# The first four output blocks of a decoder trunk, row tile by row tile

## The chip, the core and the metric

The kernel runs on one core of a Trainium2 chip. Its engines run beside each other and wait for one another through semaphores: TensorE (PE) multiplies, VectorE (DVE) and ScalarE (ACT) do elementwise work, GpSimd (POOL) some more of it, and SyncE (SP) mostly issues transfers. The metric is the device time of one execution in microseconds (us), the median of several runs. Lower is better.

## What is computed

A small hybrid decoder trunk on 256 tokens of width 2048, batch 1: a recurrent block (RG-LRU), an MLP, an attention block with three dilations, and a second MLP, each behind an RMS norm and with a residual add, and a final norm. Cut to what stands around the change:

```python
def reference(x, mix_norm, mlp_norm, final_norm, mlp_w1, mlp_w2, lru_w_in, ...):
    for i in range(DEPTH):                       # 2
        h = _rmsnorm(x, mix_norm[i])
        if i % N_MIXERS == 0:
            x = x + _rglru_block(h, lru_w_in[j], ...)
        else:
            x = x + _dilated_attention_block(h, ...)
        x = x + _mlp(_rmsnorm(x, mlp_norm[i]), mlp_w1[i], mlp_w2[i])
    return _rmsnorm(x, final_norm)

def _rglru_block(h, w_in, ...):
    xg = jnp.einsum('bsd,de->bse', h, w_in)      # 2048 -> 5120
    xb, gb = xg[..., :D_RNN], xg[..., D_RNN:]
    ...

def _rmsnorm(x, g):
    y = x32 * lax.rsqrt(jnp.mean(x32 * x32, axis=-1, keepdims=True) + EPS)
    return (y * g).astype(x.dtype)
```

The change concerns the first of these products: four blocks of 128 output channels of `w_in` applied to the normed tokens.

## The kernel before

**Three products for one.** Float32 factors are split in two: a high part, rounded for the fast matmul format, and a low part, the rest. A product of a weight block and tokens is hi x hi + hi x lo + lo x hi, three matmuls into the same PSUM bank. The high part of a weight piece is cut by ScalarE (`hi_piece`, line 132), the low part by VectorE, which needs the high part first (`lo_piece`, line 136). The tokens are split in the same way, multiplied by the norm's weight on the way (lines 1097 and 1098). The factor 1/rms of a token comes only after the product, so the products can start before the squares of the tokens are summed.

**Units.** Weights come in units of 128 x 2048 floats (1 MB), numbered in order of use, through three `raw` buffers. A transfer into a `raw` buffer waits until the low part of the unit three before it is cut. `LOOK_HI`, `LOOK_LO` and `LOOK_LOAD` set how far ahead of TensorE a unit is cut and loaded.

**The start.** Units 0 to 3 are special: `w_first` holds, for each of four chunks of 512 input channels, the weights of all four blocks (`FIRST = 4`). Within a chunk they lie block by block, each with its four row tiles of 128 input channels, so that a piece of 512 columns is one block's share of the chunk. The loop of lines 1068 to 1103 goes over the chunks: it loads 512 channels of the transposed tokens into `xg` (two buffers, `new_xg`) and the chunk's weights into `raw`, cuts them in the order that `order` gives (in chunks 1 to 3 three token tiles, a weight piece, the fourth token tile, the other three pieces), and multiplies block by block (`stand_w`: for each of the four row tiles of the block three matmuls of 256 columns). In chunk 0 tokens come in two transfers and weights in four, later the tokens in one and the weights in two. The first weight piece is issued on ScalarE's queue, all other transfers here on SP's, in program order: half of chunk 0's tokens, `par` (all small parameters, the norm's weights among them), the other half, the three remaining weight pieces, then chunk 1, 2, 3, then `con`, units 4 and 5, and the tokens in plain layout (`xc`). While the first transfers are on their way TensorE does `WARM` products of zeros (`junk`).

**Behind it.** Units 4 and 5 (line 1110), the squares of the tokens (`square_sum`, line 270) and 1/rms (`rstd_cols`, lines 277 to 284) follow. In the middle of unit 5, after `HEAD` row tiles, TensorE spreads 1/rms over the partitions (`rstd_rows`, line 291), ScalarE copies it (`rstdB`, line 294), and the finished banks of the first five blocks are scaled by VectorE (lines 426 and 454). Unit 6 is cut in halves, and then the steady run through the units begins, with the convolution (lines 433 and 437) and the gates of the recurrent block beside it. ScalarE and VectorE work strictly in program order.

Of the kernel before, what the change touches and what calls it, by code (L numbers as in the profile page):

```python
# [10 lines left out]
F32 = mybir.dt.float32  # L11
F32R = mybir.dt.float32r
AF = mybir.ActivationFunctionType
OP = mybir.AluOpType
# [3 lines left out]
S = 256  # L18
# [7 lines left out]
KD = D // 128  # L26
KR = DR // 128
# [22 lines left out]
FIRST = 4  # L50
HEAD = 14

WARM = 10
LOOK_LO = 2
LOOK_HI = 3

# [20 lines left out]
def trunk(ctx: ExitStack, tc: tile.TileContext, a: dict, out: bass.AP):  # L77
# [46 lines left out]
    def new_hi(i):  # L124
        split[i] = (cut_tile(i, "hi", HI_BUFS),)
# [4 lines left out]
    def hi_piece(i, n):  # L130
        s, r = raw[i][n]
        nc.scalar.activation(split[i][0][:, s], r, AF.Copy)  # L132

    def lo_piece(i, n):
        s, r = raw[i][n]
        nc.vector.tensor_sub(split[i][1][:, s], r, split[i][0][:, s].bitcast(F32))  # L136
# [71 lines left out]
    def pcol(name, j):  # L208
        at = PC[name][0] + j
        return par[:, at:at + 1]  # L210
# [44 lines left out]
    def halves(x):  # L255
        return x.rearrange("p (t q) -> p t q", t=2)

    def part(x, u):


        return x.rearrange("p k (t u q) -> p u k t q", t=2, u=2)[:, u]
# [39 lines left out]
    def stand_w(ps, u, ks, w_at, first, last):  # L301
        hi, lo = split[u]
        cut = 128 if state.pop("kick", False) else 256
        for j, k in enumerate(ks):
            x = xT(k)
            s = slice((w_at + j) * 128, (w_at + j + 1) * 128)
            xh, xl = moving(x, 0), moving(x, 1)
            for at in range(0, 256, cut):
                mm(ps[:, at:at + cut], hi[:, s], xh[:, at // 2:(at + cut) // 2], first and j + at == 0, False)
            cut = 256  # L310
            mm(ps, hi[:, s], xl, False, False)
            mm(ps, lo[:, s], xh, False, last and j == len(ks) - 1)
# [37 lines left out]
    def acc_tile():  # L350
        return psum.tile([P, 512], F32, name="acc", bufs=4)
# [699 lines left out]


    w = wts.tile([P, UW], F32, name="raw", bufs=RAW_BUFS)
    nc.scalar.dma_start(w[:, 0:512], units[0]["ap"][:, 0:512])
    warm = perm.tile([P, 1], F32, name="warm")
    ones = perm.tile([P, 1], F32, name="ones")
    root = perm.tile([P, 1], F32, name="root")
    nc.vector.memset(warm, 0.0)
    nc.vector.memset(ones, 1.0)
    nc.scalar.activation(warm, warm, AF.Exp)  # L1060
    zero = perm.tile([P, 512], mybir.dt.bfloat16, name="junk")
    nc.vector.memset(zero, 0.0)
    idle = psum.tile([P, 512], F32, name="g", bufs=2)
    for _ in range(WARM):
        mm(idle, zero[:, 0:128], zero, True, True)
    for m in range(FIRST):
        first[m] += (acc_tile(),)
    for n in range(NCH):
        x = new_xg(n)
        t = new_xT(n)  # L1070
        if n:
            w = wts.tile([P, UW], F32, name="raw", bufs=RAW_BUFS)
        parts = [slice(m * 512, (m + 1) * 512) for m in range(FIRST)]
        raw[n] = [(s, w[:, s]) for s in parts]
        cols = [slice(0, 2), slice(2, 4)] if n == 0 else [slice(0, 4)]
        loads = parts if n == 0 else [slice(0, 1024), slice(1024, 2048)]
        for i in range(max(len(cols), len(loads))):
            if i < len(cols):
                c = cols[i]
                nc.sync.dma_start(x[:, c, :], a["xT"][:, 4 * n + c.start:4 * n + c.stop, :])  # L1080
            if n or i:
                nc.sync.dma_start(w[:, loads[i]], units[n]["ap"][:, loads[i]])
            else:
                nc.sync.dma_start(par, a["par"])
        new_hi(n)
        new_lo(n)
        order = ("x0", "w0", "x1", "x2", "x3", "w1", "w2", "w3") if n == 0 else (
            "x0", "x1", "x2", "w0", "x3", "w1", "w2", "w3")
        for what in order:
            k = int(what[1])  # L1090
            if what[0] == "w":
                hi_piece(n, k)
                lo_piece(n, k)
                continue
            g = pcol("mix0", 4 * n + k)
            high, low = (part(t, u)[:, k] for u in range(2))
            nc.scalar.activation(high, halves(x[:, k, :]), AF.Identity, scale=g)
            nc.vector.scalar_tensor_tensor(low, halves(x[:, k, :]), g, high.bitcast(F32),
                                           op0=OP.mult, op1=OP.subtract)
        for m in range(FIRST):  # L1100
            stand_w(first[m][3][:, :S], n, range(4 * n, 4 * n + 4), 4 * m, n == 0, n == NCH - 1)
        if n == 1:
            softplus_parts()
    soft = softplus_steps()
# [77 lines left out]
def _layout(x, mix_norm, mlp_norm, final_norm, mlp_w1, mlp_w2, lru_w_in, lru_conv_w, lru_conv_b,  # L1182
# [3 lines left out]
    def cols(v):  # L1186
        return np.asarray(v).reshape(-1, 128).T
# [10 lines left out]
    def turned(w):  # L1198
# [4 lines left out]
    con, rope = _tables()  # L1203
    x2 = x[0]
    w_in = stand(lru_w_in[0])
    begin = w_in[[0, 1, KR, KR + 1]].reshape(4, 128, NCH, 512).transpose(2, 1, 0, 3)
    d = {
        "x": c(x2.reshape(NT, 128, D).transpose(1, 0, 2)),
        "xT": c(x2.T.reshape(KD, 128, 128, 2).transpose(1, 0, 3, 2)).reshape(128, KD, S),
        "par": c(np.concatenate([cols(mix_norm[0]), cols(mix_norm[1]), cols(mlp_norm[0]), cols(mlp_norm[1]),  # L1210
                                 cols(lru_lambda[0]), cols(lru_b_a[0]), cols(lru_b_x[0]), cols(lru_conv_b[0]),
                                 cols(lru_conv_w[0])], 1)),
        "con": con,
        "rope": rope,
        "g_fin": c(final_norm.reshape(1, D)),
# [28 lines left out]
```

## Time and profile before

| | us |
|---|---|
| median of 3 runs | 2014.77 |
| lowest, highest | 2014.06, 2015.1 |
| the profiled execution | 2014.87 |
| its span in the profile | 2013.1 |
| TensorE busy in the span | 2001.9 |

The span goes from the first to the last instruction of the program; the rest of an execution's time lies around it. In the views below, a row of a timeline gives start, duration, engine, line, operation, the tile written and those read, the shapes and how many instructions are merged; in brackets the idle time before it and what ended it. PE is a matmul, PEld the load of its weights, SPq and ACTq the issue of a transfer on that engine's queue. A row of the chain that ended last gives start, duration and what the chain went through. A row of the waits gives total, count and longest. A row of a transfer's view gives size and time from issue to landing. A row of the windows gives the stretch, then the busy time (and the number of instructions) of PE, PEld, DVE, ACT and POOL, the granted clock, the share of the transfer engines and GB/s.

### The profile page before, as it was taken

How to read it: one execution, taken by the hardware profiler on the slowest of the kernel's cores; microseconds unless marked ns; L12 is line 12 of the kernel's file. 1: busy time of each engine (PE TensorE's matmuls, PEld its weight loads, DVE VectorE, ACT ScalarE, POOL GpSimd, SP SyncE). 2: the span in 40 equal slices, each digit the busy share in tenths (PEclk: the TensorE clock that was granted, in tenths of full speed). 3: DMA queues.
4: the chain of work that ended last, by engine and by line, in shares of the span. 5: the costliest groups of instructions: out<-in, count | busy, mean ns of one | idle time of the engine just before them, and what ended most of it. 6: DMA issues, size and time to landing. Idle time of an engine off the chain costs nothing.

```text
span 2013.1 us, 32932 instructions
## 1 busy us (share of the span) xinstructions
PE 2001.9 (99%) x13761; PEld 1876.5 (93%) x13761; DVE 1721.5 (86%) x1903; ACT 1294.2 (64%) x1420; POOL 87.9 (4%) x83
## 2 busy tenths in 40 slices
PE   9999999999999999999999999999999999999998
PEld 8999988999999999999889999889999999999997
DVE  7999865699999999998658969857999999999985
ACT  7878875566566666665657657656666666666664
POOL 0111110000000000000000000000000000000001
PEclk9999999999999999999999999999999999999999
DMA  8555565688788788787555555456887887887774
GB/s 311 205 195 201 190 225 189 244 258 251 251 287 264 234 288 274 247 250 250 201 210 180 184 194 179 177 194 245 251 251 258 287 269 226 294 276 243 251 242 164
DMA packets 68917, 472.54 MB, mean 235 GB/s; under 512 B 7584, under 2 KB 7712, under 8 KB 13472
## 3 DMA queue, kind: packets, MB, share of 16 engines
q1 hardware_dynamic: 60416, 411.18, 54.3%
q0 software_dynamic: 8064, 58.72, 14.8%
q8 instruction: 108, 1.77, 0.3%
q10 hardware_dynamic: 288, 0.52, 0.1%
q14 instruction: 41, 0.34, 0.0%
HBM read 409.58 MB, written 2.10 MB: 205 GB/s over the span
## 4 chain that ended last, share of the span: by engine, by line
PE 96%; DVE 3%; ACT 0%; issue 0%; DMA 0%; SPq 0%; ACTq 0%
PE acc L201 46%; PE g L201 32%; PE tr L201 18%; DVE wlo L136 1%; PE tr L242 1%; DVE c L437 0%; DMA raw<-in_w_first 0%; ACT whi L132 0%; PE tr L855 0%; DVE c L433 0%; DVE sT L625 0%; DVE qT L682 0%; DVE gw L462 0%; ACT xc L973 0%; DVE i L515 0%
## 5 line engine op out<-in xcount | busy, mean ns | idle before, releaser
L132 ACT ACTIVATE whi<-raw 128x2048 fp32r<-128x2048 f32 (+1 forms) x309 | 568.9, 1844 | 308.8 <-PE acc L201 166.1
L136 DVE TENSOR_TENSOR wlo<-raw,whi 128x2048 fp32r<-128x2048 f32 (+1 forms) x309 | 677.7, 2196 | 94.3 <-ACT whi L132 94.0
L201 PE MATMUL g<-xT,whi 128*128 128x256 f32 x3649 | 617.0, 275 | 0.0
L201 PEld LDWEIGHTS g<-xT,whi 128*128 128x128 f32 x3649 | 554.0, 192 | 0.0
L201 PE MATMUL g<-xT,wlo 128*128 128x256 f32 x1824 | 502.9, 276 | 0.2 <-DVE wlo L136 0.2
L201 PE MATMUL acc<-xT,whi 128*128 128x256 f32 (+1 forms) x2212 | 455.3, 300 | 0.7 <-ACT whi L132 0.7
L201 PE MATMUL acc<-xT,wlo 128*128 128x256 f32 x1360 | 373.3, 274 | 0.7 <-DVE wlo L136 0.6
L201 PEld LDWEIGHTS acc<-xT,whi 128*128 128x128 f32 x2212 | 355.5, 191 | 15.1 <-ACT whi L132 1.8
L201 PEld LDWEIGHTS g<-xT,wlo 128*128 128x128 f32 x1824 | 350.1, 192 | 1.5 <-DVE wlo L136 0.4
L201 PE MATMUL acc<-whi,aT 128*128 128x512 f32 (+1 forms) x1086 | 322.9, 374 | 0.0
L136 DVE TENSOR_TENSOR wlo<-q,whi 128x2048 fp32r<-128x2048 f32 x112 | 255.9, 2285 | 28.0 <-ACT whi L132 27.8
L132 ACT ACTIVATE whi<-q 128x2048 fp32r<-128x2048 f32 x112 | 214.6, 1917 | 79.4 <-PE g L201 52.3
L201 PEld LDWEIGHTS acc<-xT,wlo 128*128 128x128 f32 x1360 | 261.1, 192 | 1.6 <-DVE wlo L136 1.5
L201 PEld LDWEIGHTS acc<-whi,aT 128*128 128x128 f32 x1086 | 204.0, 189 | 27.6
L201 PE MATMUL tr<-whi,sT 128*128 128x512 f32 (+1 forms) x728 | 212.7, 364 | 0.0
L201 PE MATMUL acc<-wlo,aT 128*128 128x512 f32 (+1 forms) x536 | 200.8, 376 | 0.0
L132 ACT ACTIVATE whi<-qT 128x2048 fp32r<-128x2048 f32 x56 | 107.5, 1919 | 127.8 <-PE g L201 93.3
L201 PEld LDWEIGHTS tr<-whi,sT 128*128 128x128 f32 x728 | 137.6, 189 | 20.5
L201 PE MATMUL tr<-whi,aT 128*128 128x512 f32 (+1 forms) x462 | 140.3, 373 | 0.0
L136 DVE TENSOR_TENSOR wlo<-qT,whi 128x2048 fp32r<-128x2048 f32 x56 | 128.0, 2286 | 1.3 <-ACT whi L132 1.3
L201 PE MATMUL tr<-wlo,sT 128*128 128x512 f32 x336 | 127.4, 379 | 0.0
L201 PEld LDWEIGHTS acc<-wlo,aT 128*128 128x128 f32 x536 | 101.1, 189 | 13.2
(170 smaller groups left out, 2144.4 us busy)
## 6 DMA issues: line engine op xcount, KB each, us to landing
raw<-in_w SPq DMA_DIRECT2D x172, 1024.0 KB, 7.0
q<-in_w SPq DMA_DIRECT2D x84, 1024.0 KB, 8.1
raw<-in_w_in SPq DMA_DIRECT2D x35, 1024.0 KB, 4.8
raw<-in_w_qk SPq DMA_DIRECT2D x32, 1024.0 KB, 4.8
q<-q POOLq DMA_DIRECT2D x28, 1024.0 KB, 12.5
q<-qT POOLq DMA_DIRECT2D x28, 1024.0 KB, 7.6
raw<-in_w_out SPq DMA_DIRECT2D x20, 1024.0 KB, 4.8
raw<-in_w_v SPq DMA_DIRECT2D x16, 1024.0 KB, 4.8
```

What stands on the lines that cost most here:

```text
L132: nc.scalar.activation(split[i][0][:, s], r, AF.Copy)
L136: nc.vector.tensor_sub(split[i][1][:, s], r, split[i][0][:, s].bitcast(F32))
L201: nc.tensor.matmul(o, l, r, start=start, stop=stop, skip_group_check=True)
L242: nc.tensor.transpose(tr[:, k, t * 128:(t + 1) * 128], xc[n][:, t, c:c + 128], ident)
```

## The change

The weights of the first four blocks are laid out row tile by row tile: a piece of 512 columns now holds one row tile of all four blocks. A new input `begin` (128 x 272) holds the norm's 16 columns of weights and the first row tile of tokens. It is the first transfer on SP's queue, into a tile that is otherwise used much later (`aT15`). Chunk 0's other tokens come in three transfers, each ahead of its row tile's weights; `par` moves behind the weights of chunk 1. In every chunk, a token tile is cut, then the weights of its row tile, then their products for all four blocks (first hi x hi of the four, then hi x lo, then lo x hi). The first weight piece is cut in two halves. There is one warm-up product fewer, and the zeros for it are written first.

```diff
-WARM = 10
+WARM = 9
...
     w = wts.tile([P, UW], F32, name="raw", bufs=RAW_BUFS)
+    begin = perm.tile([P, 512], F32, name="aT15")[:, 0:KD + S]
+    gains = begin[:, 0:KD]
+    nc.sync.dma_start(begin, a["begin"])
     nc.scalar.dma_start(w[:, 0:512], units[0]["ap"][:, 0:512])
     warm = perm.tile([P, 1], F32, name="warm")
     ones = perm.tile([P, 1], F32, name="ones")
     root = perm.tile([P, 1], F32, name="root")
+    zero = perm.tile([P, 512], mybir.dt.bfloat16, name="junk")
+    nc.vector.memset(zero, 0.0)
     nc.vector.memset(warm, 0.0)
     nc.vector.memset(ones, 1.0)
     nc.scalar.activation(warm, warm, AF.Exp)
-    zero = perm.tile([P, 512], mybir.dt.bfloat16, name="junk")
-    nc.vector.memset(zero, 0.0)
...
+    def part_of_tokens(n, k, x, t):
+        g = gains[:, 4 * n + k:4 * n + k + 1]
+        high, low = (part(t, u)[:, k] for u in range(2))
+        nc.scalar.activation(high, halves(x), AF.Identity, scale=g)
+        nc.vector.scalar_tensor_tensor(low, halves(x), g, high.bitcast(F32), op0=OP.mult, op1=OP.subtract)
+
+    def products(n, k, parts):
+        hi, lo = split[n]
+        xh, xl = (moving(xT(4 * n + k), u) for u in range(2))
+        for w, x in parts:
+            for m in range(FIRST):
+                s = slice((4 * k + m) * 128, (4 * k + m + 1) * 128)
+                mm(first[m][3][:, :S], (lo if w else hi)[:, s], xl if x else xh, n + k + w + x == 0,
+                   n == NCH - 1 and k == 3 and w == 1)
+
     for n in range(NCH):
         x = new_xg(n)
         t = new_xT(n)
         if n:
             w = wts.tile([P, UW], F32, name="raw", bufs=RAW_BUFS)
-        parts = [slice(m * 512, (m + 1) * 512) for m in range(FIRST)]
-        raw[n] = [(s, w[:, s]) for s in parts]
-        cols = [slice(0, 2), slice(2, 4)] if n == 0 else [slice(0, 4)]
-        loads = parts if n == 0 else [slice(0, 1024), slice(1024, 2048)]
-        for i in range(max(len(cols), len(loads))):
-            if i < len(cols):
-                c = cols[i]
-                nc.sync.dma_start(x[:, c, :], a["xT"][:, 4 * n + c.start:4 * n + c.stop, :])
-            if n or i:
-                nc.sync.dma_start(w[:, loads[i]], units[n]["ap"][:, loads[i]])
-            else:
+            nc.sync.dma_start(x, a["xT"][:, 4 * n:4 * n + 4, :])
+        xs = [begin[:, KD:] if n + k == 0 else x[:, k, :] for k in range(4)]
+        if n == 0:
+            for k in range(1, 4):
+                nc.sync.dma_start(x[:, k, :], a["xT"][:, k, :])
+                nc.sync.dma_start(w[:, k * 512:(k + 1) * 512], units[0]["ap"][:, k * 512:(k + 1) * 512])
+        else:
+            for k in range(0, 4, 2):
+                nc.sync.dma_start(w[:, k * 512:(k + 2) * 512], units[n]["ap"][:, k * 512:(k + 2) * 512])
+            if n == 1:
                 nc.sync.dma_start(par, a["par"])
+        cuts = [slice(c, c + 256) for c in (0, 256)] if n == 0 else [slice(0, 512)]
+        cuts += [slice(k * 512, (k + 1) * 512) for k in range(1, 4)]
+        raw[n] = [(s, w[:, s]) for s in cuts]
         new_hi(n)
         new_lo(n)
-        order = ("x0", "w0", "x1", "x2", "x3", "w1", "w2", "w3") if n == 0 else (
-            "x0", "x1", "x2", "w0", "x3", "w1", "w2", "w3")
-        for what in order:
-            k = int(what[1])
-            if what[0] == "w":
-                hi_piece(n, k)
-                lo_piece(n, k)
-                continue
...
-        for m in range(FIRST):
-            stand_w(first[m][3][:, :S], n, range(4 * n, 4 * n + 4), 4 * m, n == 0, n == NCH - 1)
+        at = 0
+        for k in range(4):
+            part_of_tokens(n, k, xs[k], t)
+            for _ in range(2 if n + k == 0 else 1):
+                hi_piece(n, at)
+                lo_piece(n, at)
+                at += 1
+            products(n, k, ((0, 0), (0, 1), (1, 0)))
...
-    begin = w_in[[0, 1, KR, KR + 1]].reshape(4, 128, NCH, 512).transpose(2, 1, 0, 3)
+    begin = w_in[[0, 1, KR, KR + 1]].reshape(4, 128, NCH, 4, 128).transpose(2, 1, 3, 0, 4)
...
+        "begin": c(np.concatenate([cols(mix_norm[0]), x2.T[:128].reshape(128, 128, 2).transpose(0, 2, 1).reshape(128, S)], 1)),
```

More of the change, by code (lines that the diff above doesn't have):

```diff
@@ L1085, in trunk @@
+        cuts += [slice(k * 512, (k + 1) * 512) for k in range(1, 4)]
+        raw[n] = [(s, w[:, s]) for s in cuts]
         new_hi(n)
         new_lo(n)
-        order = ("x0", "w0", "x1", "x2", "x3", "w1", "w2", "w3") if n == 0 else (
-            "x0", "x1", "x2", "w0", "x3", "w1", "w2", "w3")
-        for what in order:
-            k = int(what[1])
-            if what[0] == "w":
-                hi_piece(n, k)
-                lo_piece(n, k)
-                continue
[L1095 to L1099, printed above, removed]
```

## The prediction

> **What bounds it now.** I read the page first, then the chain that ended last, then the queues that feed its first 80 us.
>
> ```profile
> span 2013.1 us, 32932 instructions
> PE 2001.9 (99%) x13761; PEld 1876.5 (93%) x13761; DVE 1721.5 (86%) x1903; ACT 1294.2 (64%) x1420; POOL 87.9 (4%) x83
> ```
>
> TensorE idles about 11 us in all, so the change can only win or lose in stretches where TensorE waits. The chain up to 31 us, and TensorE's own timeline:
>
> ```profile
> 8.17 0.64 ACT whi L132
> ...
> 8.83 0.70 DVE wlo L136
> ...
> 9.58 20.14 PE acc L201 x178
> ```
> ```profile
> 1.25 4.45 PE L201 MATMUL g<-junk 128*128 128x512 bf16 x10 [1.25 <-DVE junk L1062]
> 6.06 0.79 PE L201 MATMUL acc<-xT,whi 128*128 128x256 f32 x2 [0.36 <-ACT whi L132]
> ```
>
> The four blocks are 4 chunks x 4 blocks x 4 row tiles x 3 = 192 products. The first 14 are spread over 6.06 to 9.58 with waits for weights; the other 178 run unbroken to 29.72. Going back from there, chunks 1 to 3 (144 products) began near 29.72 - 144 x 0.112 = 13.6. That chain seems to say: start sooner, end sooner. The next stretch of it says otherwise:
>
> ```profile
> 29.72 10.05 PE g L201 x90
> 39.77 0.23 PE tr L291 x2
> ...
> 40.02 0.38 ACT rstdB L294
> 40.41 1.82 ACT whi L132
> ...
> 42.25 2.29 DVE wlo L136
> ...
> 77.07 2.28 DVE wlo L136
> ...
> 79.40 2.61 PE acc L201 x21
> ```
>
> One product is 10.05 / 90 = 0.112 us. From 42.25 to 79.35 the chain lies almost wholly on VectorE, and TensorE waits at its end. So what counts is when VectorE reaches 42.25, and its inputs come down a second path, beside TensorE's (ScalarE's and VectorE's timelines):
>
> ```profile
> 25.16 1.91 ACT L132 ACTIVATE whi<-raw 128x2048 fp32r<-128x2048 f32 x1 [1.99 <-DMA raw<-in_w_in]
> 27.09 1.28 ACT L1112 ACT_TABLE_LOAD   x1
> ...
> 30.30 0.61 ACT L270 ACTIVATE junk<-xc 128x512 bf16<-128x512 f32 x1
> ...
> 36.72 0.20 ACT L279 ACTIVATE rs<-rs 128x2 f32<-128x2 f32 x1 [0.43 <-DVE rs L278]
> ```
> ```profile
> 27.11 2.29 DVE L136 TENSOR_TENSOR wlo<-raw,whi 128x2048 fp32r<-128x2048 f32 x1 [2.97 <-ACT whi L132]
> ...
> 37.91 2.36 DVE L136 TENSOR_TENSOR wlo<-raw,whi 128x1024 fp32r<-128x1024 f32 x2
> ```
>
> Unit 4, the first block behind the four, lands at 25.1; from then ScalarE is packed (split of unit 4, table load, split of unit 5, eight squares, root), and VectorE's low part of unit 6 ends at 37.91 + 2.36 = 40.27. The row of rstd on ScalarE ends at 40.40. The two paths meet within 0.13 us: TensorE's (transposes at 39.77) and the transfers' (unit 4 at 25.1). An earlier TensorE alone wins 0.13 to 0.2 us. Before that, the low part of unit 4 is ready at 27.11 + 2.29 = 29.40, and TensorE wants it with its third product, at about 29.8.
>
> When does unit 4 land? The rows of SP's queue (issue time first), the queue's own waits, the landings, and the bytes in the first 16 us:
>
> ```profile
> 4.73 1.01 SPq L1082 DMA_DIRECT2D raw<-in_w_first  x2
> 7.95 0.33 SPq L1080 DMA_DIRECT2D xg<-in_xT  x1
> ...
> 13.82 0.33 SPq L1080 DMA_DIRECT2D xg<-in_xT  x1
> ...
> 15.67 0.50 SPq L111 DMA_DIRECT2D raw<-in_w_in  x1
> ```
> ```profile
> SPq L1080 <- DVE xT L1098: 5.1, 2, 3.0
> ```
> ```profile
> 0.74 0.41 ACTq L1054 DMA_DIRECT2D raw<-in_w_first  x1
> ```
> ```profile
> raw<-in_w_first ACTq DMA_DIRECT2D x1, 256.0 KB, 4.0
> ```
> ```profile
> raw<-in_w_first SPq DMA_DIRECT2D x1, 512.0 KB, 7.3
> ```
> ```profile
> raw<-in_w_in SPq DMA_DIRECT2D x1, 1024.0 KB, 9.4
> ```
> ```profile
> DMA packets 1892, 4.94 MB, mean 309 GB/s; under 512 B 203, under 2 KB 331, under 8 KB 1892
> ```
> ```profile
> 14.00:16.00 2.00, 2.00 (x20) 2.00 (x20) 2.00 (x5) 1.97 (x8) 0.00 (x0) 1.00 1.01 395
> ```
>
> The first weight piece (issued 0.74 on ScalarE's queue) lands at 4.7, chunk 1's first half at 4.73 + 7.3 = 12.0, unit 4 at 15.67 + 9.4 = 25.1. In 14 to 16 us the transfer engines are full (share 1.01): unit 4's landing is set by the bytes ahead of it, as long as the queue never runs dry. The loads of tokens for chunks 2 and 3 are issued at 7.95 and 13.82, held back by VectorE's last low part of the tokens two chunks earlier (two `xg` buffers).
>
> **The change.** *Start.* 136 KB of tokens and norm weights come first, `par` goes behind chunk 1. The first weight piece still sets the start: 4.7, half a piece on ScalarE (under 0.6 us, below) makes 5.2. Nine warm-up products at 4.45 / 10 us end at 1.1 + 4.0 = 5.1. TensorE begins near 5.3 instead of 6.06 and needs only row tile 0 of all blocks. The extra instruction of the halved piece (about 0.2 us each on ScalarE and VectorE) lies beside transfers.
>
> *Chunk 0.* A row tile is 12 products = 1.34 us, and 0.39 MB of loads, about 1.3 us at the 309 GB/s above. It should end near 11.4 instead of 13.6. *Chunk 1* then waits for bytes: 2.63 MB instead of 2.73 MB lie ahead of its first half's end (`par` is behind), 0.1 MB / 0.395 = 0.25 us, so 11.8. With the split of one piece (0.63 below) its first product goes at 12.45: **1.2 us earlier**. 144 products of 0.112 later TensorE stands before unit 4 at 28.5.
>
> *There the gain ends.* With unit 4 landing as before, its low part comes at 29.40: 0.4 us of the 1.2 are left, and at 40.3 at most 0.2. The stall costs nothing by itself; late next is VectorE's chain. So at TensorE's end the change is worth 0 to -0.2 us, whatever the first 10 us do (they have 0.9 us to spare). What remains is whether unit 4 lands at 25.1.
>
> *The queue.* Each chunk's fourth token tile used to be cut after one weight piece; now it is cut after three. Durations from chunk 1, before:
>
> ```profile
> 12.04 0.63 ACT L132 ACTIVATE whi<-raw 128x512 fp32r<-128x512 f32 x1
> ...
> 12.98 1.66 ACT L132 ACTIVATE whi<-raw 128x512 fp32r<-128x512 f32 x3
> ```
> ```profile
> 12.71 0.69 DVE L136 TENSOR_TENSOR wlo<-raw,whi 128x512 fp32r<-128x512 f32 x1
> 13.31 0.48 DVE L1098 SCALAR_TENSOR_TENSOR xT<-xg,par,xT 128x256 fp32r<-128x256 f32 x1
> 13.71 1.89 DVE L136 TENSOR_TENSOR wlo<-raw,whi 128x512 fp32r<-128x512 f32 x3
> ```
>
> From start to start a weight piece takes VectorE 0.6 us and a token tile 0.4. New order in chunk 1: landing 11.8, high part to 12.45, then on VectorE low piece, tile, piece, tile, piece, tile: 3 x 0.6 + 2 x 0.4 + 0.48 = 3.1, so the buffer is free at 15.6, not 13.79. Chunk 3's tokens are issued then, and everything behind them on SP's queue (chunk 3's weights, `con`, units 4 and 5, `xc`). Issued before them are chunks 0 to 2 with `par` and the norm's columns: 3 x 1.573 + 0.115 + 0.008 = 4.84 MB. The trace has moved 4.94 MB at 16.0, so 4.84 at 15.75. How fast an empty queue answers:
>
> ```profile
> 1.00:1.50 0.50, 0.25 (x1) 0.13 (x2) 0.20 (x1) 0.32 (x1) 0.00 (x0) 1.00 0.00 0
> 1.50:2.00 0.50, 0.50 (x2) 0.15 (x1) 0.00 (x0) 0.50 (x1) 0.00 (x0) 1.00 0.58 61
> ```
>
> Issued at 0.74, bytes move in 1.5 to 2.0: about 1 us. So the engines stand still from 15.75 to 16.6, and with a ragged end and start I take **1.0 us** (bounds: 0, if the tile is cut a microsecond sooner, to 1.8, if chunk 1 lands later than 12.5). Chunk 2's tokens do not suffer: issued before row tile 3's products, near 10.0 for 7.95, when 3.27 MB are issued and 4.94 - 6 x 0.395 = 2.6 moved. Unit 4's buffer (chunk 1's weights) is free at 16.2 instead of 15.6, behind the others on SP anyway.
>
> *Sum.* Unit 4 lands at 26.1, its low part comes at 30.4; TensorE stalls from 28.7 for 1.7 us and goes on 0.6 us later than before. ScalarE's packed stretch and VectorE's unit 6 shift by 1.0, to 41.3; rstd's row follows TensorE (40.6 to 41.0) and is not the last. The chain's 42.25 becomes 1.0 - 0.2 = 0.8 later, and so do 79.4 and the end. The profiled execution took 2014.87 (span 2013.1 and 1.8 around it), 0.1 above the median 2014.77: 2014.77 + 0.8 = **2015.6**.
>
> **Rivals.** *The queue doesn't run dry* (the fourth tile's cut by 14.6, a microsecond sooner): unit 4 at 25.1, time -0.2 to +0.1, 2014.7. For it: the estimate of 15.6 hangs on one landing. Against: four VectorE instructions more (two pieces, two tiles) now stand between that landing and the tile.
>
> *The head's gain arrives in full*: 2014.77 - 1.2 = 2013.6. It needs VectorE's and ScalarE's path to come 1 us sooner too, so unit 4 at 24.1, which full transfer engines speak against.
>
> *Small loads slow the stream.* The tokens of chunk 0 now come in 128 KB loads.
>
> ```profile
> 4.00:6.00 2.00, 1.70 (x4) 0.30 (x2) 0.48 (x1) 1.02 (x3) 0.00 (x0) 1.00 0.98 298
> 5.50:6.00 0.50, 0.20 (x1) 0.00 (x0) 0.48 (x1) 0.50 (x2) 0.00 (x0) 1.00 0.96 205
> ```
>
> If these 0.53 MB go at 205 GB/s instead of 298, that is 2.6 for 1.8 us; all later bytes shift by 0.8: 2016.4. The Trainium skill, "DMA: Bandwidth & Descriptors", section "Rules for kernel authors", asks for 1 MiB a transfer and calls those under 64 KB mostly overhead. The row of 4 to 6 us, with loads of 112 to 256 KB in flight at 298 GB/s, speaks only weakly for it.
>
> *Slower: the clock falls back.* Warm-up products take 4.45 / 10 = 0.445 us for 512 columns, later ones 0.112 for 256: half the rate (the windows' clock column reads 1.00 in both, so only durations tell). The slow stretch at the start lasted 6.06 - 1.25 = 4.8 us at least and 9.58 - 1.25 = 8.3 at most. Should the 1.7 us stall at unit 4 throw TensorE back for 4.8 us, it loses 2.4, of which 0.4 is covered by unit 6's low part: 0.8 + 2.0 = 2017.6; with 8.3 us, 2019.3. It decides from a delay of TensorE over 0.4 us. Against it: no row of this trace shows a stall that long, and so no fall. The Trainium skill, "TensorE: Matmul & The Clock Gate", Part 1, puts the fall after about 3.4 us of idleness; by that, this rival would not come.
>
> **Numbers.** Forecast 0.5; no dry queue 0.2; full gain 0.1; small loads 0.12; clock 0.08. The forecast's own range: 0 to 1.8 us of dry queue, minus 0.2, 2014.6 to 2016.4; to hold 8 in 10 it goes to 2013.6 (full gain) and 2016.8 (small loads with measurement's spread, 0.5 either way). A measurement here tells about 0.2% (4.0 us) from no change; only the clock's upper end passes it: faster 0.01, same 0.96, slower 0.03.
>
> **What would show it.** Right: first products near 5.3, chunk 1 near 12.5; chunk 3's tokens issued near 15.6; a gap in transfers near 16 to 16.8; unit 4's split starting near 26.1; a TensorE wait for `wlo` of 1 to 2 us near 28.7; unit 6's low part ending near 41.3; the product of 79.40 near 80.2. Wrong: no gap near 16, or unit 4 split by 25.3, or TensorE first behind unit 6's low part.

## The result, and the profile after

| | before | after |
|---|---|---|
| median, us | 2014.77 | 2018.23 |
| lowest to highest (runs) | 2014.06 to 2016.14 (13) | 2016.98 to 2020.28 (13) |
| ratio after / before | | 1.0018 [1.0011, 1.0026] |
| the profiled execution, us | 2014.87 | 2018.45 |
| its span, us | 2013.1 | 2016.7 |

The changed kernel is slower by 3.46 us in the medians and by 3.58 in the two profiled executions. That lies outside the predicted range (2013.6 to 2016.8).

The chain that ended last, after (start, duration, what it went through):

```profile
4.55 8.24 DMA raw<-in_w_first
...
12.81 0.64 ACT whi L132
...
13.47 0.69 DVE wlo L136
14.17 0.39 DVE xT L1076
...
16.16 0.41 DVE xT L1076
16.59 0.33 SPq L1092
...
16.96 7.68 DMA raw<-in_w_first
...
24.75 0.64 ACT whi L132
...
29.11 1.91 ACT whi L132
...
31.04 2.30 DVE wlo L136
...
33.38 10.09 PE g L201 x88
...
45.98 2.29 DVE wlo L136
...
83.17 21.48 PE acc L201 x190
```

Before, this chain was TensorE's from 9.58 to 39.77. Now it runs through a transfer: VectorE's cut of chunk 1's fourth token tile (16.16) lets SP issue chunk 3's tokens (16.59), chunk 3's weights land 7.68 us after their issue, and VectorE's work on chunk 3 ends as unit 4's split begins (29.11 in the chain, 29.09 in ScalarE's timeline). That last link is the chain's guess; below, unit 4's own landing releases the split. Before, the split began at 25.16. SP's timeline and its waits, after:

```profile
9.23 0.33 SPq L1092 DMA_DIRECT2D xg<-in_xT  x1
...
16.59 0.33 SPq L1092 DMA_DIRECT2D xg<-in_xT  x1
16.96 1.55 SPq L1100 DMA_DIRECT2D raw<-in_w_first  x2
18.55 0.43 SPq L1119 DMA_DIRECT2D con<-in_con  x1
19.08 2.59 SPq L111 DMA_DIRECT2D raw<-in_w_in  x2
```
```profile
SPq L1092 <- DVE xT L1076: 6.4, 2, 5.0
```

The two waits of SP for VectorE to free `xg` take 6.4 us (5.1 before), the longer one 5.0 (3.0 before). What the transfers did meanwhile, in the windows of after (the last two columns are the share of the transfer engines and GB/s):

```profile
14.00:15.50 1.50, 1.50 (x16) 1.50 (x16) 1.50 (x5) 1.50 (x4) 0.00 (x0) 1.00 1.02 418
15.50:16.00 0.50, 0.50 (x7) 0.50 (x6) 0.50 (x2) 0.50 (x2) 0.00 (x0) 1.00 0.51 205
16.00:17.00 1.00, 1.00 (x11) 1.00 (x11) 1.00 (x3) 0.97 (x6) 0.00 (x0) 1.00 0.25 94
17.00:18.00 1.00, 1.00 (x11) 1.00 (x11) 0.97 (x3) 1.00 (x4) 0.00 (x0) 1.00 0.64 90
18.00:19.00 1.00, 1.00 (x12) 1.00 (x11) 1.00 (x3) 1.00 (x3) 0.00 (x0) 1.00 0.68 258
19.00:20.00 1.00, 1.00 (x12) 1.00 (x11) 1.00 (x3) 1.00 (x3) 0.00 (x0) 1.00 0.78 262
20.00:22.00 2.00, 2.00 (x21) 2.00 (x20) 1.34 (x4) 0.87 (x2) 0.00 (x0) 1.00 0.69 193
22.00:24.00 2.00, 2.00 (x21) 2.00 (x20) 0.46 (x1) 0.00 (x0) 0.00 (x0) 1.00 0.92 310
24.00:26.00 2.00, 1.05 (x10) 0.86 (x9) 0.59 (x1) 1.25 (x3) 0.00 (x0) 1.00 1.06 433
```

The queue is empty from about 15.75, as forecast, but full speed is back only near 24. At full engines (share 1.0) the same rows give about 420 GB/s. Unit 4's transfer and where TensorE waits (the transfers issued between 16.5 and 20 with KB and time to landing; then TensorE's timeline):

```profile
raw<-in_w_in SPq DMA_DIRECT2D x1, 1024.0 KB, 9.9
```
```profile
13.49 1.16 PE L201 MATMUL acc<-xT,whi 128*128 128x256 f32 x8 [2.42 <-ACT whi L132]
...
25.43 1.16 PE L201 MATMUL acc<-xT,whi 128*128 128x256 f32 x8 [0.95 <-ACT whi L132]
...
33.38 0.38 PE L201 MATMUL g<-xT,wlo 128*128 128x256 f32 x1 [1.84 <-DVE wlo L136]
```

Unit 4 lands at 19.08 + 9.9 = 28.98, and its split begins 0.11 later (29.09). Before it was 15.67 + 9.4 = 25.07 and 25.16, so the split waits for this landing. That VectorE's work on chunk 3 ends in the same tenth of a microsecond is chance (shown below with e10). From there everything is late by nearly one amount: unit 4's split by 3.93 (29.09 against 25.16), VectorE's 42.25 by 3.73 (45.98), the end of its chain by 3.77 (83.17 against 79.40). Behind that point nothing changed: 2018.45 - 83.17 = 1935.3, before 2014.87 - 79.40 = 1935.5. The whole loss arises before unit 4's split.

### The profile page after: what moved, and what is told of

Its sections match the earlier page's. It is cut to its first block, busy times and chain, and to the rows that moved or that the text cites. A ratio compares the mean times of both kernels' runs of the same rounds, so it can differ in the third digit from the quotient of the medians.

```text
span 2016.7 us, 32935 instructions
## 1 busy us (share of the span) xinstructions
PE 2001.3 (99%) x13760; PEld 1876.2 (93%) x13760; DVE 1721.4 (85%) x1904; ACT 1294.7 (64%) x1421; POOL 87.7 (4%) x83
## 4 chain that ended last, share of the span: by engine, by line
PE 95%; DVE 3%; DMA 1%; ACT 1%; issue 0%; SPq 0%; ACTq 0%
PE acc L201 44%; PE g L201 32%; PE tr L201 18%; DVE wlo L136 2%; DMA raw<-in_w_first 1%; PE tr L242 1%; ACT whi L132 0%; DVE c L437 0%; PE tr L855 0%; DVE c L433 0%; DVE sT L625 0%; DVE xT L1076 0%; DVE qT L682 0%; DVE gw L462 0%; ACT xc L973 0%
## 5 line engine op out<-in xcount | busy, mean ns | idle before, releaser
L132 ACT ACTIVATE whi<-raw 128x2048 fp32r<-128x2048 f32 (+3 forms) x310 | 569.9, 1840 | 309.3 <-PE acc L201 165.5
L136 DVE TENSOR_TENSOR wlo<-raw,whi 128x2048 fp32r<-128x2048 f32 (+3 forms) x310 | 678.4, 2190 | 95.6 <-ACT whi L132 95.5
L201 PE MATMUL acc<-xT,whi 128*128 128x256 f32 (+1 forms) x2212 | 450.3, 300 | 3.5 <-ACT whi L132 3.5
L201 PEld LDWEIGHTS acc<-xT,whi 128*128 128x128 f32 x2212 | 350.8, 191 | 17.9 <-ACT whi L132 4.7
L201 PE MATMUL acc<-xT,wlo 128*128 128x256 f32 x1360 | 365.2, 274 | 0.5 <-DVE wlo L136 0.3
```

What stands on the lines that cost most here:

```text
L201: nc.tensor.matmul(o, l, r, start=start, stop=stop, skip_group_check=True)
```

## The experiments

In all of them, "split" is the start of unit 4's high part on ScalarE in the profiled execution, and times in brackets are the range of the runs. The kernel before was timed again beside each group: medians 2015.36 (e1 to e4), 2015.16 (e5 to e8), 2015.07 (e9 to e11), 2015.03 (e12, e13) and 2015.56 (e14 to e16). A ratio is always to the kernel before of the same group.

**Is it the wait for the token buffer? e1** gives the tokens of chunks 2 and 3 tiles of their own that are free at that time (a chunk then comes in two loads of 256 KB), so that no load of tokens waits for VectorE:

```diff
-        x = new_xg(n)
+        if n < 2:
+            x = new_xg(n)
+            rows = [x[:, k, :] for k in range(4)]
+        else:
+            free = [perm.tile([P, 512], F32, name=f"aT{18 - 2 * n - h}") for h in range(2)]
+            rows = [f[:, at:at + S] for f in free for at in (0, S)]
...
+                for h in range(2):
+                    nc.sync.dma_start(free[h].rearrange("p (k s) -> p k s", k=2),
+                                      a["xT"][:, 4 * n + 2 * h:4 * n + 2 * h + 2, :])
...
```

> The changed kernel, but chunks 2 and 3 put their tokens into tiles that are free until much later, so no load of tokens waits for VectorE. Theory of the dry queue: chunk 3's tokens are issued before 13, no gap in the transfers near 16, unit 4 split from 25.0 to 26.0 (29.1 in the changed kernel), the end near 2014.8 (2014.3 to 2015.8). Rival, the order by row tiles or the small first loads cost the time themselves: unit 4 stays near 28 to 29 and the end near 2018.

Measured: 2014.09 (2013.79 to 2017.24), ratio 0.9995 [0.9986, 1.0004]. Chunk 3's tokens go out at 9.53. Windows of e1, then ScalarE's timeline:

```profile
16.00:17.00 1.00, 1.00 (x11) 1.00 (x11) 0.91 (x3) 1.00 (x4) 0.00 (x0) 1.00 1.07 404
17.00:18.00 1.00, 1.00 (x11) 1.00 (x11) 1.00 (x3) 1.00 (x4) 0.00 (x0) 1.00 1.10 420
```
```profile
24.88 1.91 ACT L132 ACTIVATE whi<-raw 128x2048 fp32r<-128x2048 f32 x1 [0.98 <-DVE wlo L136]
```

No gap, and the loss is gone, with the row-tile order left as it is.

**e3** is the counter-test: the kernel before, with only that wait put in. A copy of one column on VectorE reads chunk 1's last token tile behind its last weight piece:

```diff
+        if n == 1:
+            held = x
+        if n == 1:
+            nc.vector.tensor_copy(warm, held[:, 3, 0:1])
         for m in range(FIRST):
             stand_w(first[m][3][:, :S], n, range(4 * n, 4 * n + 4), 4 * m, n == 0, n == NCH - 1)
```

> The kernel before, with one tiny VectorE copy that reads chunk 1's last token tile behind that chunk's last weight piece, so the buffer comes free at 15.7 instead of 13.8; nothing else of the change. Theory of the dry queue: chunk 3's tokens are issued at 15.7, the transfers dip near 16 to 16.7, unit 4 is split 1 to 2.5 us later than 25.2 and the end comes 0.8 to 2.5 us later than before. Rival (the queue's gap costs nothing, the change costs by its head): the end as before, within 0.3 us.

Measured: 2018.01 (2015.94 to 2019.4), ratio 1.0013 [1.0004, 1.0021]. Tokens issued at 15.56; windows of e3, then ScalarE's timeline:

```profile
15.50:16.00 0.50, 0.50 (x7) 0.50 (x6) 0.50 (x2) 0.50 (x2) 0.00 (x0) 1.00 0.30 123
16.00:17.00 1.00, 1.00 (x11) 1.00 (x11) 0.99 (x3) 1.00 (x4) 0.00 (x0) 1.00 0.57 94
17.00:18.00 1.00, 1.00 (x12) 1.00 (x11) 1.00 (x3) 1.00 (x3) 0.00 (x0) 1.00 0.90 328
18.00:19.00 1.00, 1.00 (x12) 1.00 (x11) 1.00 (x3) 0.62 (x2) 0.00 (x0) 1.00 0.55 152
19.00:20.00 1.00, 1.00 (x12) 1.00 (x11) 0.57 (x1) 0.14 (x1) 0.00 (x0) 1.00 0.91 106
```
```profile
28.14 1.91 ACT L132 ACTIVATE whi<-raw 128x2048 fp32r<-128x2048 f32 x1 [2.20 <-DMA raw<-in_w_in]
```

The same gap, the same slow recovery and most of the loss (2.65 us, a little above the 2.5 that was expected at most; the change cost 3.46 and, timed again as e16, 2.81), in a kernel with none of the change's reordering. Taking the wait away removes the loss, putting it in makes most of it: this is the cause.

**e8** gives the kernel before the free tiles too (the edit of e1 in its loop).

> The kernel before with chunks 2 and 3 loaded into free tiles, nothing else of the change. Theory that TensorE's earlier start is covered: as fast as the changed kernel with free tiles, 2014.1 (2013.6 to 2014.7), TensorE unbroken up to unit 4. Rival, the order by row tiles wins something once the queue does not run dry: 0.5 us or more above the changed kernel with free tiles, 2014.7 to 2015.3.

Measured: 2014.6 (2013.98 to 2015.26), ratio 0.9996 [0.9987, 1.0005]; split at 24.33, but 1/rms's row reached ScalarE later (40.16 in e8, 39.51 in e1), so there TensorE is the later path. Against e1's -1.27 to its own before, e8 has -0.56: with the queue full the row-tile order is worth about 0.7 us in the medians, which these intervals can't tell from nothing.

**How the size depends on the time of issue.** e5 and e6 are e1 with chunk 3's first token tile written by a one-column memset on VectorE first, behind chunk 1's or chunk 2's second low piece, so that its transfer is held to that point:

```diff
+    late = [perm.tile([P, 512], F32, name=f"aT{12 - h}") for h in range(2)]    # chunk 3's tokens
...
+            if (n, k) == (1, 1):     # e6: (2, 1)
+                nc.vector.memset(late[0][:, 0:1], 0.0)
             products(n, k, ((0, 0), (0, 1), (1, 0)))
```

> The kernel with free tiles, its first load of chunk 3's tokens held by a one-column VectorE memset until chunk 1's second low weight piece is cut, about 13.6 (9.5 when free; 13.8 in the kernel before). 0.8 MB still wait then, so the queue does not run dry. Theory, only a dry queue costs: unit 4 split within 0.5 us of the 24.9 of the free tiles, the end 2013.8 to 2015. Rival, a shallow queue is slow too (the kernel before moved only 320 KB/us from 16 to 21, the free tiles 390): 300 to 350 KB/us after 16, unit 4 split 25.2 to 26, the end 0.3 to 1 us later.

> The same with the memset behind chunk 2's second low weight piece, about 17.8, 1.2 us later than chunk 3's tokens were issued in the changed kernel (16.6). Theory of the dry queue: a gap from 15.8 to 18.8, then a slow restart as in the changed kernel; unit 4 split near 30.2 (29.1 in the changed kernel), the end near 2019.3. Rival, the delay is not proportional to the gap (the order by row tiles costs): 2014 to 2016.

Measured: e5 2015.83 (2015.28 to 2018.64), ratio 1.0004 [0.9995, 1.0013]; e6 2020.93 (2020.67 to 2022.6), ratio 1.0030 [1.0018, 1.0042]. In e5 the hold let go at 14.78 rather than 13.6, since chunk 1 itself landed late (12.35). The window of e5 from 1 to 7 us after that issue:

```profile
15.78:21.78 6.00, 6.00 (x56) 6.00 (x56) 5.45 (x11) 4.53 (x12) 0.00 (x0) 1.00 0.88 285
```

So e5 is slow without a gap: from 15 to 21.5 us the rate falls below 209 GB/s in no half microsecond, and yet the split comes 1.7 us later than before. Its rival, that a queue with little in it is slow too, came nearer than its theory, that only a dry queue costs. Seven of the profiled executions side by side:

| kernel | chunk 3's tokens issued | split | profiled time | time - split |
|---|---|---|---|---|
| e1 | 9.53 | 24.88 | 2014.0 | 1989.1 |
| before | 13.82 | 25.16 | 2014.87 | 1989.7 |
| e5 | 14.78 | 26.84 | 2015.87 | 1989.0 |
| e3 | 15.56 | 28.14 | 2017.24 | 1989.1 |
| after | 16.59 | 29.09 | 2018.45 | 1989.4 |
| after again (e16) | 17.56 | 28.36 | 2017.74 | 1989.4 |
| e6 | 18.83 | 30.01 | 2020.67 | 1990.7 |

From e1 to e16 the time follows the split of unit 4 within 0.7 us, and the split follows the issue: up to about 13.8 it costs next to nothing, from there to 16.59 the split moves 3.9 us for 2.8. The second profile of the changed kernel stands out of the line: issued a microsecond later than in the first, but behind a quicker recovery (309 GB/s for 237 from 1 to 7 us after the issue, see below). (e6's extra 1.3 us is another thing, in the last section.)

**e2**, the change with all four token tiles of chunks 1 to 3 cut ahead of the weights, was to free `xg` early by order alone:

```diff
+        if n:
+            for k in range(4):
+                part_of_tokens(n, k, xs[k], t)
         for k in range(4):
-            part_of_tokens(n, k, xs[k], t)
+            if n == 0:
+                part_of_tokens(n, k, xs[k], t)
```

> The changed kernel, but in chunks 1 to 3 all four token tiles are cut ahead of the chunk's weights; layout, loads and products as changed. Theory of the dry queue: chunk 1's tokens land near 11.5, their last low part is cut by 13.8, chunk 3's tokens are issued then as in the kernel before, no gap near 16, the end 2014.3 to 2016. Rival, the cost lies in layout, loads or the order of the products: 2018.

Measured: 2014.78 (2013.8 to 2017.49), ratio 0.9998 [0.9989, 1.0007]. It wins back the loss in the median, though its profiled execution (2017.14) lies near the top of that range: there the tokens went out at 14.43, the split came at 26.74, and TensorE's clock fell (last section).

**Can something else fill the gap? e4** issues `con` and the first quarter of `xc` ahead of chunk 3's tokens:

```diff
+            if n == 3:
+                nc.sync.dma_start(con, a["con"])
+                nc.sync.dma_start(xc[0], a["x"][:, :, 0:512])
             nc.sync.dma_start(x, a["xT"][:, 4 * n:4 * n + 4, :])
...
-    nc.sync.dma_start(con, a["con"])
...
-    for n in range(NCH):
+    for n in range(1, NCH):
```

> The changed kernel, but con and the first of the four loads of plain tokens (0.79 MB, they wait for nothing) are issued ahead of chunk 3's tokens, so that the queue has work in the gap. Theory of the dry queue with a slow restart: no gap, chunk 3 and unit 4 go at the rate of the kernel before, unit 4 split near 26.5 to 27.5 (the 0.52 MB moved ahead cost 1.3 us), the end 2015.8 to 2017. If only bytes count and not the gap: unit 4 later than in the changed kernel by 1.3 us, the end near 2019.5.

Measured: 2017.47 (2016.19 to 2018.94), ratio 1.0009 [1.0001, 1.0018]; tokens issued at 16.24, split at 28.18. The engines are busy now (373 to 393 GB/s from 16 to 18), with bytes that nobody waits for; chunk 3 is about as late as in the changed kernel, and the time lies between the two that were expected. **e12** instead puts chunk 3's weights, whose buffer is free, ahead of the held tokens:

```diff
+            if n < 3:
+                nc.sync.dma_start(x, a["xT"][:, 4 * n:4 * n + 4, :])
...
+            if n == 3:
+                nc.sync.dma_start(x, a["xT"][:, 4 * n:4 * n + 4, :])
```

> The changed kernel, but in chunk 3 the two loads of weights stand ahead of the held load of tokens on SP's queue. The weights wait for nothing there, so 1 MB fills the gap and only the tokens (0.5 MB) come late. Theory of the dry queue: no gap near 16 to 18, unit 4 split at 25.2 to 26.2 (29.1 in the changed kernel), the end 2014.3 to 2015.7. Rival, the held load of tokens delays unit 4 wherever it stands: the end 2017 or more.

Measured: 2015.97 (2014.5 to 2018.62), ratio 1.0003 [0.9994, 1.0012]; split near 26.7, both a little later than expected. Most of the loss is won back. What remains is that chunk 3's tokens still come late, and ScalarE cuts them in front of unit 4.

**Why is the queue slow behind the gap?** The prediction let it go on at full rate. Three guesses at the reason: packet size, any restart, the token load. **e10** loads chunk 3's weights in one 1 MB transfer:

```diff
-            for k in range(0, 4, 2):
+            wide = 4 if n == 3 else 2
+            for k in range(0, 4, wide):
...
```

> The changed kernel, but chunk 3's weights come in one load of 1 MB (8 KB packets) for two of 0.5 MB (4 KB packets); its tokens are held back by the buffer as before. If small packets behind an empty queue are what is slow: 350 to 420 KB/us from 19 on (205 to 283 from 19 to 23 in the changed kernel), unit 4 split near 27.5 (29.1), the end near 2016.7. If not the size of the packets but the empty queue is: rates as in the changed kernel, the end near 2018.2.

Measured: 2016.54 (2014.8 to 2018.52), ratio 1.0008 [0.9999, 1.0017]; in its profile 258, 205, 233 and 270 GB/s in the four microseconds from 18 to 22, split near 29.3. In this profile larger packets do not cure it. But this execution (2018.52) was the slowest of the eleven, and the median is the one that was expected if packet size mattered (2016.7, for 2018.2 otherwise); so packet size may be a part of it, and that stays open. **e7** (e1, with `con` held behind chunk 3's second low piece) and **e13** (e1, with only chunk 3's weights held) make a gap of the same kind in front of other transfers:

```diff
+            if (n, k) == (3, 1):                       # e7
+                nc.vector.memset(con[:, 0:1], 0.0)
-            w = wts.tile([P, UW], F32, name="raw", bufs=RAW_BUFS)    # e13
+            w = late if n == 3 else wts.tile([P, UW], F32, name="raw", bufs=RAW_BUFS)
...
+            if (n, k) == (2, 1):
+                late = wts.tile([P, UW], F32, name="raw", bufs=RAW_BUFS)
+                nc.vector.memset(late[:, 0:1], 0.0)
```

> The kernel with free tiles, but con, and with it units 4 and 5 behind it, held by a one-column memset of con behind chunk 3's second low weight piece, about 22.9. The queue runs dry near 19.7, with 8 KB packets behind the gap instead of 4 KB. If any restart from an empty queue is slow: 200 to 280 KB/us in the 4 us from 24 to 28, unit 4 split 30.5 to 31.5, the end near 2020. If only chunk 3's data or those microseconds were slow: 380 to 420 KB/us from 24.5, unit 4 split 28 to 28.7, the end near 2018.

> The kernel with free tiles, chunk 3's tokens early, its weights alone held by a one-column memset behind chunk 2's second low weight piece (the same point as the run that held tokens and weights, 18.8 there). The queue runs dry near 17 instead of 15.8. If the weights move at 380 to 420 KB/us from 20.5 on, the tokens were what moved slowly behind a gap: unit 4 split near 27.5, the end near 2017. If the weights move at 220 to 320 KB/us, whatever of chunk 3 comes behind a gap is slow: unit 4 split 28.5 to 29.5, the end 2018.5 to 2019.5.

Measured: e7 2019.36 (2018.29 to 2020.5), ratio 1.0021 [1.0012, 1.0030]; e13 2018.16 (2016.8 to 2019.02), ratio 1.0014 [1.0005, 1.0023]. To compare, the windows from 1 to 7 us after the issue of the first held transfer, in after, e7, e13 and, where nothing was held, e1 at the same place:

```profile
17.59:23.59 6.00, 6.00 (x56) 6.00 (x55) 4.18 (x9) 3.28 (x8) 0.00 (x0) 1.00 0.78 237
```
```profile
24.25:30.25 6.00, 5.42 (x49) 5.22 (x47) 0.96 (x2) 1.47 (x1) 0.00 (x0) 1.00 1.00 377
```
```profile
20.35:26.35 6.00, 6.00 (x56) 6.00 (x56) 3.55 (x8) 3.25 (x8) 0.00 (x0) 1.00 0.97 348
```
```profile
16.00:22.00 6.00, 6.00 (x56) 6.00 (x56) 4.92 (x11) 4.73 (x12) 0.00 (x0) 1.00 1.05 416
```

Six microseconds at 237 instead of 416 GB/s are 6 x (1 - 237/416) = 2.6 us of full work lost. The same window gives 235 in e3, 252 in e10, 291 in e6 and 309 in e16: all those with the tokens at the head of the emptied queue and the old layout stay under 310, the two with something else reach 348 and 377. Cut in halves, the first three microseconds do not separate them (195 to 299 GB/s with the tokens at the head, 283 in e13, 342 in e7), the last three do: 244 in after, 318 in e16, 274 in e3, 286 in e10, 309 in e6, against 414 in e13 and 412 in e7. So a recovery this slow is not a rule of every restart; in these profiles it goes with the tokens. It does not hit the tokens alone: in after they land 4.8 us after their issue, and chunk 3's first weights (24.64) 3.2 us behind them, though the load has the same size. In e1's window chunk 3's tokens still move at first (they land at 17.39 and 18.07), at 404 and 420 GB/s, then weights and `con`. **e14** is the change with the transposed tokens laid out chunk by chunk in memory, so that each chunk is one stretch; **e15** is e1 with the same layout:

```diff
-        "xT": c(x2.T.reshape(KD, 128, 128, 2).transpose(1, 0, 3, 2)).reshape(128, KD, S),
+        "xT": c(x2.T.reshape(KD, 128, 128, 2).transpose(1, 0, 3, 2)
+                .reshape(128, NCH, 4, S).transpose(1, 0, 2, 3)),
...
```

> The changed kernel, but the transposed tokens lie in memory chunk by chunk, so that a chunk's load reads 512 KB in one stretch and not 128 rows of 4 KB at a pitch of 16 KB. Loads, waits and order as changed. If the pitch is what makes the held tokens slow: over 330 KB/us from 18.5 on, the tokens land within 3.5 us of their issue (4.8 in the changed kernel), unit 4 split near 27.5 (29.1), the end near 2016.7. If not: 200 to 280 KB/us from 19 to 23 again, the end as the changed kernel in the same call (2017.5 to 2018.5).

> Free tiles for chunks 2 and 3 and the tokens chunk by chunk in memory. If the pitch slows transfers even without a gap: chunk 1 lands sooner than 11.2, unit 4 split before 24.5, the end 2013.5 to 2014. If not: as the free tiles alone, 2014.1 to 2014.8.

> The changed kernel as it is, beside the two. Theory: chunk 3's tokens are issued at 16 to 17 again, a gap follows, the end 2017 to 2019, 2 to 4 us above the kernel before in the same call. A second profile shows how much chunk 1's landing (12.8 in the first) and the rate behind the gap vary.

Measured, in one group with the unaltered changed kernel (e16, 2018.37, 2017.0 to 2019.58, ratio 1.0012 [1.0003, 1.0020]): e14 2016.7 (2015.58 to 2018.08), ratio 1.0006 [0.9997, 1.0015]; e15 2014.59 (2013.42 to 2016.29), ratio 0.9995 [0.9986, 1.0004]. The window of e14 from 1 to 7 us after the issue (15.53):

```profile
16.53:22.53 6.00, 6.00 (x56) 6.00 (x56) 4.62 (x10) 4.39 (x11) 0.00 (x0) 1.00 0.96 323
```

The layout gives back 1.67 us in the medians (2018.37 - 2016.7). In the two profiles this comes from the earlier issue, not from the recovery: chunk 1 landed at 11.74 for 13.76, the tokens went out at 15.53 for 17.56, and from there to the split it is 10.8 us in both (323 GB/s and 309). The held tokens land 4.3 us after their issue in both, not within the 3.5 that the pitch as the reason would have asked for. In e15, without a gap, it gives nothing that the intervals show. So how the tokens lie in memory is part of the size, not the cause.

**Two tries to gain more.** e9 is e1 with 13 warm-up products instead of 9; e11 is e1 with units 4 and 5 loaded in halves:

```diff
-WARM = 9
+WARM = 13                                              # e9
-    load(4)
-    load(5)
+    load(4, 1024)                                      # e11
+    load(5, 1024)
```

> The changed kernel with free tiles and 13 warm-up products for 9, so TensorE's real products begin 1.7 us later at first and less once the clock is up. Theory, what TensorE wins in the first 10 us is given back at the wait for chunk 1 (11.9 in the free tiles): the first product of chunk 1 within 0.3 us of 12, the end 2014.1, unchanged within 0.4. Rival, an early start reaches the end: 1 to 1.7 us later, 2015.1 to 2015.8.

> The changed kernel with free tiles, units 4 and 5 loaded and cut in halves, so that ScalarE can begin with half a unit. On the theory that behind unit 4 ScalarE's and VectorE's packed stretch sets the end: unit 4's split begins near 24.0 for 24.9, unit 6's low part ends 0.4 to 0.7 us sooner than 39.9, the end near 2013.6 (0.5 less). Rival, TensorE is the later of the two there: no change, 2014.1.

Measured: e9 2014.76 (2014.02 to 2016.79), ratio 1.0000 [0.9991, 1.0009]; e11 2014.77 (2013.44 to 2016.28), ratio 0.9998 [0.9989, 1.0007]. e9 did not test what it was meant to: in its profile the first real product comes at 5.19 for 4.86 in e1, and chunk 0 is done at 11.17 for 10.93, so the start moved by 0.3 us and not by 1.7. Against its own before e9 has -0.31, e1 -1.27, and the intervals overlap; in the profiles chunk 1 landed at 12.02 in e9 and at 11.22 in e1. Halves change nothing that can be measured (unit 6's low part ends at 39.93 for 39.98 in e1). No version clearly beats the kernel before; e1 and e15 (0.9995 [0.9986, 1.0004] both) lie below the changed one (1.0018 [1.0011, 1.0026]).

## Why the prediction was right about the cause and wrong about the size

- **The head**: right. First product at 4.88 for 5.3 forecast, chunk 0's last products end at 11.1 (10.47 + 0.61) for 11.4, and none of it reaches the end measurably (e8).
- **Chunk 1**: wrong by a microsecond. The forecast divided the bytes ahead by a full rate and got 11.8 for its landing; 12.79 was measured (13.76 in e16), later than before rather than 0.25 sooner. From 8 to 10 us the thirteen profiles with the row-tile order and the old layout of the tokens moved 237 to 336 GB/s (after: 281), the three with the old order (before, e3, e8) 365 to 416, the two with the tokens in one stretch 368 and 369. Chunk 1 landed between 11.2 and 13.8 in the thirteen, at 11.74 and 11.40 in those two. So a slower stream, which the rival "small loads slow the stream" had forecast, did come, but from 8 us on, not in the first 6, and not by that rival's reason: e14 and e15 load chunk 0's tokens in the same small loads. It goes with the row-tile order and the scattered rows together; why chunk 1's token load costs nothing in the old order stays open.
- **The late token tile**: right. From landing to release of the buffer the working had 0.65 + 3.1 = 3.75 us, the chain shows 16.57 - 12.79 = 3.78. With the landing a microsecond late, tokens were issued at 16.59, not 15.6.
- **"Dry 1.0 us": the step that failed.** The empty queue was forecast rightly (from about 15.75), its first bytes too (about 1 us). But the term took a queue that goes on at full rate from then on. By the forecast unit 4 lands 26.1 - 15.6 = 10.5 us after the issue of the tokens; measured, 28.98 - 16.59 = 12.4. So of the 2.9 us between the forecast +1.0 and the measured +3.9, 1.0 is chunk 1's landing and 1.9 the slow stretch behind the gap. The upper bound of 1.8 allowed for the first and not for the second. The second profile divides otherwise: in e16 the tokens go out 2.0 us later than forecast (17.56), since chunk 1 landed at 13.76, and unit 4 lands at 28.25, 10.7 us behind them, near the forecast's 10.5. So the term was too small by both, and their shares differ from one execution to the next; e5 adds that the stretch can be slow with no gap at all. Why it is slow stays open. The trace of before had a hint of it. In its own window from 1 to 7 us after the issue of chunk 3's tokens (13.82), where they were held for 3.0 us and the queue had become short,

```profile
14.82:20.82 6.00, 6.00 (x56) 6.00 (x55) 5.96 (x13) 5.40 (x14) 0.00 (x0) 1.00 0.98 335
```

the engines count as busy (0.98) and yet move 335 GB/s, not 416. A busy share is not a rate; the forecast read the rate of 14 to 16 us (395) and took it for all that follows.
- **From unit 4 to the end**: right. "Unit 4's delay minus 0.2" gives 3.93 - 0.2 = 3.73, which is what VectorE's row shows (45.98 - 42.25). TensorE's stall for `wlo` was forecast at 1.7 and is 1.84 in the bracket (the high part is ready at 31.01, as TensorE ends chunk 3 at 31.06, so TensorE waits for the low part alone).
- **Not a second path**: the chain of after ends unit 4's wait with VectorE's last low piece of chunk 3. e10 shows that the split does not need it (ScalarE's timeline, then VectorE's):

```profile
28.79 2.43 ACT L132 ACTIVATE whi<-raw 128x512 fp32r<-128x512 f32 x2
```
```profile
29.68 0.69 DVE L136 TENSOR_TENSOR wlo<-raw,whi 128x512 fp32r<-128x512 f32 x1
```

The first row holds chunk 3's last high part and unit 4's (1.91 us in the other runs), which therefore begins near 28.79 + 2.43 - 1.91 = 29.31, while VectorE's last low piece of chunk 3 ends at 30.37. There the split waits for its landing (29.03) and for ScalarE alone, as the forecast had it.
- **The other rivals**: the queue did run dry, the head's gain did not arrive, and the clock's fall was absent from the first profile of the changed kernel and present in the second, there at the wait for chunk 1 and not at the stall at unit 4 that the rival named.

## What to carry to other kernels

Transfers behind one queue are late by whatever holds the first of them: before moving a small tile's last use down in an engine's order, look for the transfer that waits for its buffer and for everything issued behind it, and give that transfer a buffer of its own (e1) or put ahead of it loads that are needed next and whose buffers are free (e12, but not e4). Price an emptied or nearly emptied queue by the rate that it has afterwards (237 and 309 GB/s for 416 over six microseconds in two executions here), not by the delay of its first byte. A path that has little slack decides what an early start is worth: the earlier start here met a transfer that could not come sooner.

## What the runs showed of the hardware

**The rate behind a late issue went with what was issued late.** From 1 to 7 us after the issue: 235 to 309 GB/s with pieces of tokens (4 KB, in e5 and e6 2 KB) that lie 16 KB apart at the head of the queue, 323 with the tokens in one stretch, 348 and 377 with weights or `con`. These are single executions. Why the scattered tokens are slow only when little is queued (in e1 chunk 3's tokens, just as scattered, go out at 9.53 into a full queue, and the stretch in which they land shows 404 and 420 GB/s) stays open.

**TensorE's clock can fall around waits of 1.8 to 3.3 us.** The clock column (third from the end) of e16 and e6 in the windows:

```profile
14.50:17.50 3.00, 3.00 (x14) 3.00 (x15) 3.00 (x7) 2.97 (x9) 0.00 (x0) 0.50 0.63 258
18.00:21.00 3.00, 3.00 (x30) 3.00 (x29) 2.97 (x7) 3.00 (x8) 0.00 (x0) 1.00 0.83 238
```
```profile
35.00:38.00 3.00, 3.00 (x17) 3.00 (x16) 2.66 (x4) 2.90 (x9) 0.00 (x0) 0.50 1.07 423
38.00:41.00 3.00, 3.00 (x27) 3.00 (x27) 2.55 (x15) 2.88 (x10) 0.00 (x0) 0.93 1.01 416
```

At 0.50 TensorE does 14 to 17 products in 3 us instead of 29 or 30. By the waits in brackets in TensorE's timelines, in e16 and e2 it came with one of 3.29 and 3.18 us for chunk 1, in e10 with one of 2.64; in e6 and e13 with one of 1.84 for unit 4's low part; in e7 between one of 1.08 and one of 1.84, and there the clock stayed low from 32 to beyond 38. The first profile of the changed kernel has waits of 2.42, 0.95 and 1.84 and no fall.

What decides is where a wait lies. The clock records of the traces begin between 4.0 and 6.8 us, and every fall begins a whole number of steps of 3.41 us later: 3 steps (10.24 us) in e2, e10 and e16, 8 (27.31) in e7 and e13, 9 (30.72) in e6. It lasts one step, in e7 two. The step ahead of the fall holds 3.28 us of waiting in e16, 2.99 in e2, 2.35 in e13, 2.33 in e10, 1.84 in e6 and 1.81 in e7. No other step in the eighteen traces holds more than 1.83, and two with 1.82 and 1.83 (e4, and e7 earlier) brought no fall. So in these traces the border lies near 1.8 us of waiting in one step. In after, 1.84 us of waiting at unit 4 (31.54 to 33.38) is cut in two by the border of a step at 32.50 and brings no fall; in e6 the same wait lies within one step.

The Trainium skill, "TensorE: Matmul & The Clock Gate", Part 1, puts the fall after about 3.4 us of idleness. e16 and e2 come near that; e6, e7, e10 and e13 speak against it as a lower limit. The prediction had used that page against this rival, and the runs do not bear it out. The price shows as in the table above: time less split is 1990.7 in e6 and in e13 (2018.98 - 28.29) and 1991.7 in e7 (2020.5 - 28.78), against 1989.0 to 1989.8 in the versions of the changed kernel without a fall near the split. That is 1 to 2.7 us, of the order that the rival on the clock had worked out. It comes through TensorE: the transposes of 1/rms follow ScalarE's row of rstd by 4.1 to 4.3 us in these three, by 2.7 in after. In e2 (1990.4) the fall ahead of the split made TensorE the later path too; in e10 and e16 (1989.2 and 1989.4) TensorE had enough time in hand ahead of unit 4 to cover it. Falls in some executions and not in others may be one reason for the changed kernel's wide spread (2016.98 to 2020.28); how much of it they make wasn't measured.
